# Spreading dense tiles and the samples' attention over the eight pairs of heads, with seven instead of four merge-gate blocks kept in DRAM

## The chip, the core and the metric

The kernel runs on one core of one Trainium2 chip. The metric is the device time of one execution in microseconds (us). The core has a matrix engine (TensorE, PE in the profile), a vector engine (DVE), a scalar engine (ACT), a general engine (POOL) and a queue engine (SP) that issues most of the transfers; each runs its own instructions strictly in the order in which they were written, and waits where an operand or a buffer isn't ready.

## What is computed

One layer of a decoder for a prompt of 512 tokens and for 8 samples with one new token and 1024 cached positions each. Two attentions run on the same input; the core of the reference is:

```python
h = x * (1.0 + scale[:, None, :]) + shift[:, None, :]
parts = jnp.split(h @ w_in, np.cumsum(IN_WIDTHS)[:-1], axis=-1)
(a_q, a_kc, a_vc, a_ks, a_vs, a_kw, a_vw, a_g, a_z, b_q, b_k, b_v, b_z, m_a, m_b) = parts
...
o_a = nsa_attention(...)    # compressed, selected and window branch, gated per head
o_b = moba_attention(...)   # blocks chosen by q . mean(k), plus the own block
y_a = (o_a.reshape(bsz, t, NSA_WIDTH) * jax.nn.silu(a_z)) @ w_up_a
y_b = (o_b.reshape(bsz, t, MOBA_WIDTH) * jax.nn.silu(b_z)) @ w_up_b
mixed = (jax.nn.sigmoid(m_a) * y_a + jax.nn.sigmoid(m_b) * y_b) @ w_out
x_new = layer_norm(DEEPNORM_ALPHA * x + gate[:, None, :] * mixed, ln_g, ln_b)
```

All numbers are f32; for the samples the keys and values come from paged caches through a page table.

## The kernel before

**Dense tiles.** The product with `w_in` is cut into tiles of 128 output columns. `dense` (L550) does one: 48 matmuls on two PSUM banks, `d<-hTh,hl` twice and `d<-hTl,hl` once for each of 16 pieces, because f32 is split into a high and a low part. The weights of a tile are one load of 512 KB (`raw<-w_cols`, L342, on SP, ring of 4 buffers), and each half is split by an ACT cast (L310) and a subtraction on DVE or POOL (L231) into `hl` (ring of 3). `SEQ` fixes the order of all tiles. Tile names: bq, bk, bv, bz are query, key, value and gate path of the second attention (0 to 3), q, z those of the first, ma and mb the two merge gates (0 to 7; "m3" means ma3 and mb3), g the output gate's four parts (each two loads `raw<-ada_g` of the same ring).

**Prompt attention.** `attend(pi)` (L1112) does the pair of heads pi of 0 to 7: `prepare` (L957) loads the bias band from `band_d`, a table in DRAM; then `score` (L1001, PE writes bank s, DVE adds the band, L1012, ACT takes the exponential, L1016), `turn` (L1021, transposes), `value` (L1035). Pairs 0 to 3 also have the compressed branch (`cmp_score`, matmuls `s<-ck,q`). `band_d` itself is written once, by one transfer of 3 MB on POOL's queue (L940), while the compression is worked out.

**The samples' attention.** `dec_a` (L1177) and `dec_b` (L1252) run through a list of loads, with two buffers: 4 items of 16 selected-key pages (`raw<-slck`, 64 KB each, L721 on SP, one transfer for each page), 2 window-key items (`wink`), 16 items of 4 pages `mobk` (256 KB each), twice two gathers of values by POOL (`slcv`) and one window-value load (`winv`), and 16 items of 4 pages `mobv` (256 KB each). An item can be loaded when the item two before it has been used.

**What sets the order.** `merge` (L177) takes generators of work and always steps the one with the smallest share done. For each pair of heads three are merged: `attend(pi)`, whose total is `ATT[pi]`, the samples' attention up to the share `DEC_SHARE[pi]`, and the dense tiles `FILLS[pi + 1]`. What is left of the samples' attention runs with `FILLS[9]` after the last pair. `FILLS[0]` goes with the compression before. The tables thus set the order of every engine's instructions, SP's loads too.

**Merge gates.** `gen_m` (L648) puts ma and mb of a block through a tanh. A block computed while the pairs of heads still run has no place in SBUF: its halves go through `mg` (two buffers) to `m_d` in DRAM (L658, 260 KB a half), and are loaded again (L1332, 520 KB a block) when the pool `fm` has been opened after pair 7. Blocks of `FILLS[9]` stay in SBUF.

Of the kernel before, what the change touches and what calls it, by code (L numbers as in the profile page):

```python
# [33 lines left out]
        + [f"{n}{t}" for t in range(4) for n in ("bq", "bz", "bv", "bk")]  # L34
        + [f"{n}{c}" for c in range(8) for n in ("ma", "mb")])
FILLS = [["ks", "vs", "ag", "vw", "q0", "bq2", "kw", "q1", "q2", "q3"],
         ["bq0", "bq1"],
         ["bq3", "bv0"],
         ["z0", "bk0", "m0"],
         ["bv1", "z1", "m1", "bv2"],  # L40
         ["bk1", "m2"],
         ["z2", "bk2", "m3"],
         ["bv3", "z3", "bk3"],
         ["bz0"],
         ["bz1", "bz3", "bz2", "g0", "m4", "g1", "g2", "m5", "m6", "g3", "m7"]]
DEC_SHARE = [0.09, 0.15, 0.28, 0.31, 0.37, 0.45, 0.52, 0.66]
DEC, DEC_PACE = 50000.0, 0.875
PHIS = 49353.58399999998
ATT = [20400, 20000, 17000, 47040, 10800, 5250, 7500, 9000]
SECOND = [3, 4, 6, 7]  # L50
LIM = 0, 384, 384, 768
NORM_N = 512
# [124 lines left out]
def merge(*flows):  # L177

    while True:
        live = [f for f in flows if f.live]  # L180
        if not live:
            return
        min(live, key=Flow.share).step()
# [7 lines left out]
def build(tc, A):  # L191
# [44 lines left out]
    with ExitStack() as es:  # L236
# [441 lines left out]
        def fill_cost(names):  # L678
            return max(1.0, sum(2 * DENSE if n[0] == "m" else 1000 if n[0] == "g" else 1700 if n == "ag" else 1 if n == "ks" else DENSE for n in names))
# [432 lines left out]
        def attend(pi):  # L1112
            js = jobs_of(pi)
            if pi < 7:
                prepare(pi + 1)
            for k, j in enumerate(js):
                ex = []
                if pi < 4 and k == 0:
                    ex = [(cmp_score, pi)]
                if pi < 4 and k == 1:  # L1120
                    ex = [(cmp_turn, pi)]
                yield from step(j, ex)
            if pi == 7:
                for _ in range(2):
                    yield from step(None)
# [187 lines left out]
        def part(until):  # L1313
            while fa.live and fa.share() < until:
                d = fa.done
                fa.step()
                yield fa.done - d

        done = 0.0
        for pi in range(8):  # L1320
            merge(Flow(attend(pi), ATT[pi]), Flow(part(DEC_SHARE[pi]), max(1.0, (DEC_SHARE[pi] - done) * DEC)),
                  Flow(fills(FILLS[pi + 1]), fill_cost(FILLS[pi + 1])))
            done = DEC_SHARE[pi]
        at_es.close()
# [370 lines left out]
```

## Time and profile before

| | |
|---|---|
| median of three runs | 663.61 us (657.27 to 663.81) |
| profiled execution | 660.91 us |
| its span | 659.1 us |
| PE busy | 619.0 us, 94% |
| DVE, ACT, POOL busy | 310.5, 295.2, 287.3 us |
| mean granted clock of TensorE | 0.974 |
| moved by DMA | 124.77 MB |

The span runs from the first to the last instruction of the profiled execution. A window gives the busy time of each engine in a stretch of it, the granted clock of TensorE there (1.00 is 2.4 GHz, 0.50 is 1.2 GHz) and the share of time in which the 16 DMA engines were at work. In a chain of waits each piece is what the next one waited for.

### The profile page before, as it was taken

The page shows a single profiled execution, that of the slowest core. Times are in us where ns is not written, and L with a number is a line of the kernel's source. Part 1 is how long each engine was busy: PE and PEld are TensorE (multiplying, and loading weights), DVE is VectorE, ACT ScalarE, POOL GpSimd, SP SyncE. Part 2 cuts the span into 40 slices and gives each one's busy share as a digit, 9 for nine tenths or more (in the row PEclk, how much of TensorE's full clock was granted, in tenths as well). Part 3 has the DMA queues.
Part 4 walks back from the last instruction along what each step waited for, and adds up shares of the span by engine and source line. Part 5 has one row for each costly group of instructions (what it writes and reads, how often), then busy time and mean ns, then how long its engine had stood idle before and what let it go on. Part 6 is the DMA issues. An engine that isn't in the chain of part 4 may idle for free.

```text
span 659.1 us, 13320 instructions
## 1 busy us (share of the span) xinstructions
PE 619.0 (94%) x4747; PEld 518.1 (79%) x4747; DVE 310.5 (47%) x800; ACT 295.2 (45%) x679; POOL 287.3 (44%) x328
## 2 busy tenths in 40 slices
PE   6999999999979799999999899998988999999993
PEld 4778999999959578776879679865635998999672
DVE  1465543532572664335355446744431145545177
ACT  2248455544443545444445446645433353433521
POOL 1105466542352433442364544445432264655746
PEclk9998999999998969999999989999998999999998
DMA  8895554539953594699775563168977344345102
GB/s 309 337 293 188 167 179 144 171 98 97 165 186 104 155 360 141 216 310 311 245 229 196 196 237 97 49 220 312 304 264 288 100 153 137 96 129 188 68 24 106
DMA packets 64132, 124.77 MB, mean 189 GB/s; under 512 B 8142, under 2 KB 28368, under 8 KB 63521
## 3 DMA queue, kind: packets, MB, share of 16 engines
q1 hardware_dynamic: 61954, 116.58, 52.9%
q0 software_dynamic: 2112, 7.34, 6.3%
q8 instruction: 37, 0.61, 0.4%
q14 instruction: 29, 0.24, 0.1%
HBM read 112.76 MB, written 11.13 MB: 188 GB/s over the span
## 4 chain that ended last, share of the span: by engine, by line
PE 66%; DMA 6%; SPq 3%; DVE 3%; issue 2%; ACT 1%; POOL 1%; POOLq 0%; ACTq 0%; DVEq 0%
PE d L199 40%; PE s L199 9%; PE e L199 7%; DMA raw<-mobv 3%; PE pt L1025 3%; SPq L721 2%; PE o L202 2%; PE o L199 2%; PE pt L199 1%; PE e L202 1%; DMA raw<-slcv,vidx 1%; DMA raw<-winv 1%; DVE xt L1488 1%; DMA craw<-cmp 1%; SPq L717 0%
## 5 line engine op out<-in xcount | busy, mean ns | idle before, releaser
L199 PE MATMUL d<-hTh,hl 128*128 128x260 f32 (+1 forms) x1408 | 273.1, 290 | 1.4 <-DVE hl L231 1.1
L199 PEld LDWEIGHTS d<-hTh,hl 128*128 128x128 f32 (+1 forms) x1408 | 221.4, 189 | 16.8 <-issue 9.4
L199 PE MATMUL d<-hTl,hl 128*128 128x260 f32 (+1 forms) x704 | 201.4, 287 | 0.0
L199 PEld LDWEIGHTS d<-hTl,hl 128*128 128x128 f32 (+1 forms) x704 | 133.2, 189 | 3.2 <-issue 2.5
L231 POOL TENSOR_TENSOR hl<-raw,hl 128x512 fp32r<-128x512 f32 x56 | 73.5, 1314 | 104.2 <-ACT hl L310 99.6
L310 ACT CAST hl<-raw 128x512 fp32r<-128x512 f32 (+1 forms) x111 | 67.8, 615 | 76.1 <-PE d L199 62.6
L1018 POOL TENSOR_SCALAR p<-p,sm,gp 128x512 f32<-128x512 f32 (+1 forms) x64 | 40.0, 626 | 95.8 <-DVE sm L1017 91.2
L1016 ACT ACTIVATE p<-s,sm 128x512 f32<-128x512 f32 (+1 forms) x96 | 50.8, 530 | 65.9 <-PE pt L1025 54.0
L231 DVE TENSOR_TENSOR hl<-raw,hl 128x512 fp32r<-128x512 f32 (+1 forms) x55 | 53.5, 974 | 49.4 <-ACT hl L310 47.6
L199 PE MATMUL d<-yh,hl 128*128 128x260 f32 x256 | 46.3, 282 | 0.0
L1025 PE MATMUL pt<-cst,p 128*128 128x128 f32 x240 | 40.3, 282 | 1.5 <-DVE pp L1030 0.8
L199 PEld LDWEIGHTS d<-yh,hl 128*128 128x128 f32 x256 | 39.7, 188 | 1.0 <-issue 0.4
L199 PE MATMUL s<-kd,q 128*128 128x512 f32 (+1 forms) x96 | 35.1, 366 | 4.6 <-ACT p L1016 4.6
L1010 DVE TENSOR_REDUCE sm<-s 128x1 f32<-128x256 f32 (+1 forms) x48 | 16.9, 354 | 44.9 <-PE s L199 43.9
L1025 PEld LDWEIGHTS pt<-cst,p 128*128 128x128 f32 x240 | 27.8, 142 | 11.5 <-issue 5.8
L1018 POOL TENSOR_SCALAR p<-p,sm,cst 128x512 f32<-128x512 f32 (+3 forms) x32 | 19.5, 611 | 38.1 <-DVE sm L1017 37.9
L199 PE MATMUL d<-yl,hl 128*128 128x260 f32 x128 | 36.0, 282 | 0.0
L199 PE MATMUL s<-u,w1h 128*128 128x256 f32 (+1 forms) x160 | 33.5, 301 | 1.2 <-ACT u L793 0.7
L1012 DVE CUSTOM_DVE_ANT_0 s<-s,band 128x256 f32<-128x256 f32 (+1 forms) x48 | 17.3, 362 | 35.2 <-PE s L199 24.8
L199 PEld LDWEIGHTS s<-kd,q 128*128 128x128 f32 x96 | 18.6, 194 | 17.8 <-ACT p L1016 8.6
L231 POOL TENSOR_TENSOR u<-craw,u 128x512 fp32r<-128x512 f32 x16 | 21.3, 1331 | 24.8 <-ACT u L828 24.8
L199 PE MATMUL s<-kd,qx 128*128 128x512 f32 (+1 forms) x96 | 31.5, 330 | 0.0
(425 smaller groups left out, 1167.3 us busy)
## 6 DMA issues: line engine op xcount, KB each, us to landing
raw<-w_cols SPq DMA_DIRECT2D x46, 512.0 KB
raw<-mobk SPq DMA_DIRECT2D x64, 256.0 KB
raw<-mobv SPq DMA_DIRECT2D x64, 256.0 KB
u<-ada_ss SPq DMA_DIRECT2D x16, 512.0 KB
craw<-cmp SPq DMA_DIRECT2D x64, 128.0 KB
raw<-slck SPq DMA_DIRECT2D x64, 64.0 KB
raw<-ada_g SPq DMA_DIRECT2D x8, 512.0 KB
raw<-w_up SPq DMA_DIRECT2D x8, 512.0 KB
```

Of the source, the lines that this page charges most:

```text
L199: i = mmraw(out, lhsT, rhs, start=start, stop=stop, skip_group_check=True)
L202: i = mmraw(out, lhsT, rhs, start=start, stop=stop, skip_group_check=True)
L231: (nc.gpsimd if eng == "p" else nc.vector).tensor_sub(out, x, f32(hi))
L310: nc.scalar.copy(h, src)
L721: dyn.append(nc.sync.dma_start(out, A[name][bass.ds(page, 1)].rearrange("a p c -> p (a c)")))
L1010: nc.vector.tensor_reduce(sm[:, 0:1], s[:, :b], axis=AX, op=OP.min)
L1012: nc.vector.tensor_tensor_reduce(out=s[:, b:n], in0=s[:, b:n], in1=j.band[:, 256 - (n - b):], scale=1.0, scalar=top, op0=OP.add, op1=OP.mi ...
L1016: nc.scalar.activation(pr, s[:, :n], AF.Exp, scale=-1.0, bias=sm[:, 1:2], accum_out=sm[:, 2:3])
L1018: nc.gpsimd.tensor_scalar(pr, pr, sm[:, 3:4], j.gate(i), op0=OP.mult, op1=OP.mult)
L1025: nc.tensor.transpose(p[:, k * 128:k * 128 + 128], j.p[i][:, kb * 128:kb * 128 + 128], ident)
L1488: add(xt[tt][:, c], xt[tt][:, c], u)
```

## The change

Three tables, and nothing else:

```diff
--- before.py
+++ after.py
@@ -34,19 +34,19 @@
         + [f"{n}{t}" for t in range(4) for n in ("bq", "bz", "bv", "bk")]
         + [f"{n}{c}" for c in range(8) for n in ("ma", "mb")])
 FILLS = [["ks", "vs", "ag", "vw", "q0", "bq2", "kw", "q1", "q2", "q3"],
-         ["bq0", "bq1"],
-         ["bq3", "bv0"],
-         ["z0", "bk0", "m0"],
-         ["bv1", "z1", "m1", "bv2"],
-         ["bk1", "m2"],
-         ["z2", "bk2", "m3"],
-         ["bv3", "z3", "bk3"],
-         ["bz0"],
-         ["bz1", "bz3", "bz2", "g0", "m4", "g1", "g2", "m5", "m6", "g3", "m7"]]
-DEC_SHARE = [0.09, 0.15, 0.28, 0.31, 0.37, 0.45, 0.52, 0.66]
+         ["bq0", "m0", "bq3", "bq1"],
+         ["bv0", "m1", "bk0", "bv1"],
+         ["z0", "m2", "m3"],
+         ["m4", "z1", "m5"],
+         ["bk1", "bv2", "z2"],
+         ["bk2", "bv3", "bk3"],
+         ["z3", "bz0"],
+         ["bz1", "m6"],
+         ["bz3", "bz2", "g0", "g1", "g2", "g3", "m7"]]
+DEC_SHARE = [0.15, 0.3, 0.44, 0.56, 0.6, 0.64, 0.74, 0.845]
 DEC, DEC_PACE = 50000.0, 0.875
 PHIS = 49353.58399999998
-ATT = [20400, 20000, 17000, 47040, 10800, 5250, 7500, 9000]
+ATT = [17100] * 4 + [7100] * 3 + [11000]
 SECOND = [3, 4, 6, 7]
 LIM = 0, 384, 384, 768
 NORM_N = 512
```

Before, blocks m0 to m3 are computed among the pairs of heads and wait in DRAM; now m0 to m6, which is six more stores `m_d<-mg` of 260 KB and three more loads of 520 KB. Of the samples' attention, 66% of the steps were done with the pairs of heads; now 84.5%. After the last pair, ten entries with bz1, bz3, bz2, four blocks of m and the gates were left; now bz3, bz2, the four gates and m7.

The order moves on all engines from the first tile after the compression on. Three places, word for word.

PE, where the first score of pair 0 stands. Names: `s<-kd,q` is a score, `s<-ck_88` the compressed branch's scores, `d<-hTh,hl` and `d<-hTl,hl` a dense tile, `e<-xc`, `e<-cvd,u` and `e<-cst_72,pr` steps of the samples' compressed branch (`dec_cmp`, L887, and `new_scores`, L872). Before:

```order
L199 MATMUL d<-hTl,hl 128x260
L199 MATMUL d<-hTh,hl 128x260 x2
L199 MATMUL d<-hTl,hl 128x260
L199 MATMUL s<-kd,q_1970 128x512
L199 MATMUL s<-ck_88,q_1970 128x64
L199 MATMUL d<-hTh,hl 128x260 x2
L199 MATMUL d<-hTl,hl 128x260
```

and in the changed program:

```order
L199 MATMUL e<-xc,cstd 128x64
L912 MATMUL e<-cst_72,xc 64x128
L199 MATMUL e<-cvd,u 128x128 x4
L199 MATMUL e<-cst_72,pr 128x1 x2
L199 MATMUL s<-kd,q_1970 128x512
L199 MATMUL s<-ck_88,q_1970 128x64
```

Before, this score stood behind five whole dense tiles and part of the sixth (bk0), counted from the compression's end, and the steps of `dec_cmp` lay apart among them; now it stands right behind these steps, with bq0, ma0 and half of mb0 ahead.

SP, at the loads of the band (L961) and of the first selected-key pages (slck). Before:

```order
L721 DMA craw<-cmp 128x256
L342 DMA raw<-w_cols 128x1024 x6
L572 DMA ok<-ev 128x520
L961 DMA band<-band_d 128x2x256 x2
L717 TENSOR_LOAD ptt
L721 ISA
L721 DMA raw<-slck 128x128
```

and in the changed program:

```order
L721 DMA craw<-cmp 128x256
L342 DMA raw<-w_cols 128x1024 x4
L961 DMA band<-band_d 128x2x256 x2
L717 TENSOR_LOAD ptt
L721 ISA
L721 DMA raw<-slck 128x128
```

Two weight loads fewer stand ahead of the band; the 64 page loads follow it directly in both, with no weight load among them.

PE, at the last value item (`e<-raw,tp`, 4 pages mobv) and the gates' matmuls (`s<-raw,cs`). Before:

```order
L199 MATMUL s<-raw,cs 32x512
L202 MATMUL s<-raw,cs 32x512 x3
L199 MATMUL e<-raw,tp 32x512
L202 MATMUL e<-raw,tp 32x512 x3
L199 MATMUL d<-hTh,hl 128x260 x2
L199 MATMUL d<-hTl,hl 128x260
```

and in the changed program, from the third gate on:

```order
L199 MATMUL s<-raw,cs 32x512
L202 MATMUL s<-raw,cs 32x512 x3
L199 MATMUL o<-pp,v_5298 64x512
L202 MATMUL o<-pp,v_5298 64x512
L202 MATMUL o<-pp,v_5298 64x384 x2
L202 MATMUL o<-pp,v_5298 64x256 x2
L202 MATMUL o<-pp,v_5298 64x128 x2
L199 MATMUL s<-raw,cs 32x512
L202 MATMUL s<-raw,cs 32x512 x3
L199 MATMUL d<-hTh,hl 128x260 x3
L199 MATMUL d<-hTl,hl 128x260
```

Before, half of mb4 and the six tiles ma5, mb5, ma6, mb6, ma7 and mb7 stood behind the last value item, with the fourth gate between mb6 and ma7; now only ma7 and mb7 do, behind pair 7's last values and the fourth gate.

## Rows read from the trace of the kernel before

**Rows 1.** Page, parts 1 and 2: TensorE's sum and its granted clock in 40 slices.

```profile
PE 619.0 (94%) x4747; PEld 518.1 (79%) x4747; DVE 310.5 (47%) x800; ACT 295.2 (45%) x679; POOL 287.3 (44%) x328
...
PEclk9998999999998969999999989999998999999998
```

**Rows 2.** Windows: length, busy us of each engine, granted clock, DMA share, GB/s.

```profile
195.80:206.00 10.20, 10.19 (x57) 8.30 (x58) 2.87 (x10) 3.08 (x8) 1.23 (x2) 0.70 0.38 107
206.00:244.00 38.00, 33.72 (x218) 25.54 (x217) 20.93 (x63) 17.11 (x46) 13.18 (x16) 0.87 0.69 235
...
360.00:400.00 40.00, 36.36 (x405) 29.50 (x405) 19.47 (x64) 19.19 (x51) 19.48 (x23) 0.96 0.61 211
...
440.00:505.00 65.00, 57.14 (x404) 31.93 (x402) 23.52 (x86) 27.42 (x76) 25.32 (x33) 0.97 0.86 299
505.00:545.80 40.80, 40.80 (x344) 39.82 (x341) 12.84 (x13) 16.73 (x34) 15.47 (x14) 1.00 0.46 152
sum 350.00, PE 334.05 PEld 261.52 DVE 158.00 ACT 165.49 POOL 141.65; mean PE 47.72 PEld 37.36 DVE 22.57 ACT 23.64 POOL 20.24
```

**Rows 3.** Groups of instructions on PE from 145.7 to 195.8: count, busy us, mean ns.

```profile
L199 PE MATMUL d<-hTh,hl 128*128 128x260 f32 x218 | 41.7, 287 | 1.1 <-DVE hl L231 1.1
L199 PE MATMUL d<-hTl,hl 128*128 128x260 f32 x109 | 30.8, 282 | 0.0
```

**Rows 4.** Tile band_d: its one issue (start us) and its time to landing.

```profile
L940 POOL DMA_DIRECT2D band_d<-bs x1: 1104/1104/1104, 146.9 to 146.9; - x1
...
DMA to landing us min/median/max: 36.5/36.5/36.5
```

**Rows 5.** Timeline of SP's queue, 140 to 232: start, us from first to last, issue.

```profile
183.49 0.90 SPq L961 DMA_DIRECT2D band<-band_d  x2
184.93 39.75 SPq L721 DMA_DIRECT2D raw<-slck  x64
...
227.03 0.43 SPq L342 DMA_DIRECT2D raw<-w_cols  x1
```

**Rows 6.** Timeline of PE, start and us: around the first page item and before z1.

```profile
195.81 1.03 PE L199 MATMUL e<-raw,zn 128*32 128x512 f32 x1 [3.50 <-DMA raw<-slck]
...
197.93 0.80 PE L199 MATMUL d<-hTh,hl 128*128 128x260 f32 x2
```

**Rows 7.** The same view, 228 to 241.

```profile
231.14 1.09 PE L199 MATMUL e<-ew 33*128 33x512 f32 x2 [2.17 <-ACT pp L1028]
...
237.25 0.78 PE L199 MATMUL d<-hTh,hl 128*128 128x260 f32 x2
```

**Rows 8.** Chain of waits, in order of time: start, us, what.

```profile
376.36 5.43 DMA raw<-slcv,vidx
...
446.31 5.88 DMA raw<-mobv
...
485.00 3.80 DMA raw<-mobv
...
495.80 8.16 DMA raw<-mobv
...
534.19 35.62 PE d L199 x288
...
577.73 10.06 PE d L199 x84
```

**Rows 9.** Windows, same columns as Rows 2: the value loads, and the band table's write.

```profile
432.50:503.60 71.10, 63.64 (x455) 37.45 (x454) 27.20 (x97) 30.40 (x82) 27.09 (x35) 0.98 0.85 293
150.00:165.00 15.00, 15.00 (x129) 14.77 (x127) 3.59 (x10) 6.52 (x17) 4.11 (x4) 1.00 0.98 97
```

**Rows 10.** Timeline of ACT, start and us: a weight split that waits for its load.

```profile
173.16 0.62 ACT L310 CAST hl<-raw 128x512 fp32r<-128x512 f32 x1 [2.06 <-DMA raw<-w_cols]
```

**Rows 11.** Page, part 5: the two halves of a weight split.

```profile
L231 POOL TENSOR_TENSOR hl<-raw,hl 128x512 fp32r<-128x512 f32 x56 | 73.5, 1314 | 104.2 <-ACT hl L310 99.6
L310 ACT CAST hl<-raw 128x512 fp32r<-128x512 f32 (+1 forms) x111 | 67.8, 615 | 76.1 <-PE d L199 62.6
```


## The prediction

> **What bounds the kernel now.** I read the page first. TensorE is busy 619.0 us of 659.1 [rows 1], so whatever this change does must be read from PE's idle stretches and from the slices in which its granted clock falls from 2.4 to 1.2 GHz. The windows come next [rows 2]: from 195.8 to 545.8 (ma7 and mb7 start at 534.19 in the chain [rows 8], and 96 of that piece's 288 matmuls later the up projections begin, which the change doesn't touch) PE is busy 334.05 of 350.0 us. So 15.95 us are idle, and nearly all of that lies in three windows: 206 to 244, 360 to 400 and 440 to 505. What the clock costs in a window is its length times what lacks of 1.00: 3.06 us in 195.8 to 206, 4.94, 1.60 and 1.95 in the three named, 11.55 in sum. That makes 27.5 us that a better order after 195.8 could win. Then the timelines and the chain say what each loss is. First, SP's queue [rows 5]: the table band_d, issued at 146.9, lands 36.5 us later [rows 4], the band loads go at 183.49, behind them 64 page loads hold SP for 39.75 us, and the next weights are issued at 227.03; z1 starts at 237.25 [rows 7]. PE runs out of dense tiles in between: it idles before 231.14 for 2.17 us, and is then at half clock (the first pieces of z1 show twice the time of two matmuls). Second, PE waits for the gathered values (376.36, 5.43 us) [rows 8]. Third, the 14 last value items come in a stretch that the DMA engines fill to 85%, at 293 GB/s [rows 9], and the chain passes from item to item: 5.88, 3.80, 8.16 us [rows 8].
>
> **What the change costs: the start.** Up to 145.7 us the programs are alike. In both, PE's first item of selected-key pages starts when its 16 page loads are there, at 195.81 [rows 6], because SP issues them only behind the band, and the band only behind band_d. Before, PE has by then done 218 + 109 = 327 dense matmuls since 145.7 [rows 3]. Counted in the changed order, 168 stand ahead of the same item: the first scores stand so early that the second one waits for a bank that comes free only when the band is there, some 10 us later. The attention done by then is the same. A dense matmul takes 10.06 / 84 = 0.120 us [rows 8], so 159 matmuls, 19.0 us, are left over. This is the one term that I read as nearly certain; PE is idle here for about that long, and all else on this engine queues behind.
>
> Two weight loads fewer stand ahead of the band. While band_d is written the engines are at work 98% of the time and move 97 GB/s [rows 9]: alone, 3 MB would take 3.146 / 0.097 = 32.4 us instead of 36.5, so the two loads can bring the band and all page loads forward by 0 to 4.1 us. I take 1.0, since some weight loads remain.
>
> Here a rule speaks on how much. ACT waits until 173.16 for a weight load [rows 10] of the time in which band_d is written, and 150 to 165 shows no more than band_d's rate [rows 9]. The Trainium skill (DMA: Bandwidth & Descriptors, Queues, rings and completion order) says that each DMA engine takes turns between the queues it has work for, packet by packet. By that rule SP's loads would get through at once and delay band_d all along, and fewer of them would give the whole 4.1 us: the sum below would end 3.1 us lower. The row, with no more than 97 GB/s moved, doesn't show the weights coming through early.
>
> **What it gives: 195.8 to 250.** The 159 matmuls now lie in the stretch where PE ran dry. Weights of seven tiles are loaded ahead of the band (two loads fewer than before, where nine were), which leaves 336 - 168 = 168 matmuls, 20.1 us, against 106 that ran in before's 195.8 to 237.25. They reach about as far as mb1's weights, the first behind the page loads, which can be ready at the 237.25 at which z1 could start. So the 4.28 us idle and 4.94 us of clock go; I leave 0 to 3 us for mb1's weights, taken with the next window. The half clock right behind the first item (3.06) stays, since PE idles longer ahead of it now.
>
> **250 to 400.** By the order, 909 dense matmuls lay between the first page item and the first of the 14 value items; now 1218. That covers more waits, among them the gathers': of 3.64 idle and 1.60 of clock I keep 1.5 (0 to 5.2). Six stores to m_d and three more loads add 3.1 MB; at 232 to 300 GB/s that is 10 to 13 us of the engines, in stretches that leave 30% and more of them free; 1.0 us for all that and mb1's weights (0 to 4).
>
> **The value items.** From the first to the last of 14 they took 71.1 us, with 132 dense matmuls among them. Now 198 lie there: 66 more, 7.9 us; some scores, values and transposes (about 5.2 us by count) moved out, so PE's work in the stretch grows by 2.7. Its work before was 63.64 busy less 1.4 of clock, 62.2, so 64.9 now. The same 14 items and about as many weight, gate and gate-block loads pass. At before's rate the stretch stays 71.1 (6.2 us lost); at a full share it needs 71.1 x 0.85 = 60.4 and PE sets it (0 lost). Items stand more evenly now, one for each 4.6 us of PE's work, near the 3.80 to 5.88 us of an item with two buffers; I take the middle, 3.0, in place of 7.86 + 1.95.
>
> **Behind the last value item.** Before, 312 dense matmuls ran here without a wait, and loads had all their time. Now the gates' loads fill the ring of four, and ma7's weights are issued only when the third gate's matmuls are done. Estimated from rows: a transfer of 3.80 to 5.88 us (chain, a value item; a weight load is half as large), ACT 0.62 and POOL 1.31 for the split [rows 11], less about 3.3 us that pair 7's values and the fourth gate take: 2.4 to 4.5. I take 3.0 (1 to 4.5).
>
> **The sum.** 350.0 + 19.0 left over - 27.5 + 3.1 (clock kept) + 1.5 + 1.0 + 3.0 + 3.0 - 1.0 = 352.1 us from 195.8 on, 2.1 us more than before. Against its own execution, 660.91, this gives 663.0. The median of the runs shown is 663.61, so it stands between; their spread of 6.5 us is about 1%, which is what a measurement of this kernel can tell from no change. All losses at their low end, with the band 4.1 early, give 350.0 + 19.0 - 27.5 + 3.1 + 1.0 - 4.1 = 341.5, so 652.4; a wait inside a started matmul counts as busy in the windows, and may hide 2 us more of gain. All at their high end: 344.6 + 5.2 + 4.0 + 6.2 + 4.5 = 364.5, so 675.4.
>
> **The rivals.** *Everything after the start is hidden.* The even order keeps PE fed to the end, band and page loads come up to 4 us earlier. For it: 309 more dense matmuls to hide waits with, and a full share of DMA that would allow 60.4 us for the value items. Against it: two buffers, and a fixed order with no slack. It gives 651 to 655. *The value items stay bound by DMA, and the start is not repaid.* One mechanism: 14 MB of values with two buffers run at no more than 293 GB/s however they are placed, so the stretch takes 71.1 us again, and its PE work, larger than before, doesn't shorten it; behind it only two tiles are left where before 312 matmuls ran, with ma7's weights late. With the gathers' wait also partly there (3), this gives 344.6 + 3 + 1 + 6.2 + 4.5 - 1 = 358.3, so 669. It decides against the change from 67 us in that stretch on. For it: 5.88, 3.80 and 8.16 us pieces of the chain. Against it: the 85% contain waits of SP for PE. *PE is late at the first page item.* ACT and DVE are held by the band too, and the splits of bq1 and bv0 stand behind their waiting instructions; if weights come 6 us late after the band, the clock stays low with them: 663 + 6 + 1.5 = 670. *The change shifts losses only* is my forecast.
>
> **How the numbers follow.** The forecast, losses moved from the end to the start and the sum within 1%, 0.44. All hidden, 0.24. DMA-bound values or a late restart, 0.32. The range leaves out 1 in 10 on each side: 651 at the low end, where the first rival reaches, and 674 near the sum of all high ends. The forecast's own range is 657 to 668. Faster by over 1%: 0.24; within 1%: 0.44; slower: 0.32.
>
> **What would show it.** PE idle for 10 us or more between 170 and 188, and a second wait before 195.8; the band's load issued at 180 to 184; no idle at 228 to 237. The first page item at 191 to 196 with 168 dense matmuls behind it; the value stretch at 65 to 71 us; a wait of ma7 for its weights; the up projections at 543 to 553. It is wrong if PE isn't stopped by the band (then the kernel is faster by up to 19 us), or if a new wait shows between 250 and 400.

## The result

The changed kernel takes 665.05 us in the median (20 runs, 662.34 to 670.07), the kernel before 661.38 us (20 runs, 654.36 to 665.69, on the same chip): a ratio of 1.0083, with 95% from 1.0059 to 1.0106. By this ratio it is 0.8% slower, some 5.5 us; the two medians lie 3.7 us apart. The forecast was 663.0 us and no difference that can be told: the time lies in the range, but the difference is there, and it is a loss. The profiled execution of the changed kernel is 663.52 us with a span of 661.8, against 660.91 and 659.1 of before.

The page of the profile after, TensorE's sum and its granted clock, as [rows 1]:

```profile
PE 617.3 (93%) x4747; PEld 517.7 (78%) x4747; DVE 311.0 (47%) x800; ACT 294.1 (44%) x679; POOL 290.7 (44%) x328
...
PEclk9999999998669999999999999999999989999997
```

The clock now falls to 0.6 in two slices of 16.5 us, from 165 to 198 us, where it was 0.9 before; the 0.6 that before had from 231 to 247 is gone. The timeline of SP's queue from 140 to 250 us of the changed kernel, as [rows 5] (start, length, and how many issues):

```profile
180.59 0.90 SPq L961 DMA_DIRECT2D band<-band_d  x2
182.05 41.33 SPq L721 DMA_DIRECT2D raw<-slck  x64
...
226.22 0.38 SPq L342 DMA_DIRECT2D raw<-w_cols  x1
```

The tile band_d of the changed kernel: its one issue, who waited for it, and its landing, as [rows 4]:

```profile
L940 POOL DMA_DIRECT2D band_d<-bs x1: 1104/1104/1104, 145.2 to 145.2; - x1
...
  ACT mg L656: 12.8, 1
  DVE s L1012: 10.0, 1
...
DMA to landing us min/median/max: 3.0/19.1/35.3
```

The write starts 1.7 us earlier than before, by a stretch in which both programs are alike, and takes 1.2 us less. The first page item of the samples' attention starts 2.5 us earlier. PE's timeline of the changed kernel from 164 to 200 us, as [rows 6] (brackets: idle time ahead, and what ended it):

```profile
168.56 0.80 PE L199 MATMUL s<-kd,q 128*128 128x512 f32 x1 [1.03 <-DVE q L970]
...
185.03 0.58 PE L199 MATMUL s<-kd,q 128*128 128x256 f32 x1 [7.33 <-ACT p L1016]
...
193.28 1.06 PE L199 MATMUL e<-raw,zn 128*32 128x512 f32 x1 [3.25 <-DMA raw<-slck]
```

The first scores (over 512 and over 384 columns) are done from 168.56 on; the third, over 256 columns at 185.03, waits until the first has got its band and gone through ACT. That is decided by the band: its loads go at 180.59, DVE's addition waits 9.97 us for them and starts at 183.55, ACT's exponential follows at 184.19. Then the page loads are waited for. Windows of the changed kernel from the first page item to the up projections, the columns of [rows 2]:

```profile
193.30:206.00 12.70, 12.70 (x81) 10.70 (x85) 4.48 (x17) 3.77 (x10) 2.22 (x4) 0.76 0.38 108
206.00:244.00 38.00, 37.74 (x288) 30.13 (x283) 19.34 (x62) 21.02 (x54) 14.87 (x17) 1.00 0.69 242
244.00:360.00 116.00, 115.94 (x949) 91.99 (x948) 52.53 (x161) 54.44 (x138) 48.30 (x55) 1.00 0.75 251
360.00:400.00 40.00, 40.00 (x416) 36.46 (x415) 17.90 (x60) 19.23 (x51) 14.91 (x20) 1.00 0.56 185
400.00:456.00 56.00, 54.18 (x429) 48.57 (x428) 33.28 (x98) 33.74 (x85) 30.31 (x35) 1.00 0.26 81
456.00:525.30 69.30, 63.98 (x483) 42.30 (x481) 25.41 (x91) 28.46 (x79) 24.61 (x33) 1.00 0.88 292
525.30:548.70 23.40, 22.15 (x161) 16.29 (x161) 11.41 (x10) 10.98 (x22) 13.27 (x11) 0.93 0.73 264
sum 355.40, PE 346.69 PEld 276.44 DVE 164.36 ACT 171.63 POOL 148.49; mean PE 49.53 PEld 39.49 DVE 23.48 ACT 24.52 POOL 21.21
```

Here 8.71 us are idle, and the clock costs 3.05 us in the first window and 1.64 in the last: 13.4 us lost, where before 27.5 were. Without the losses the stretch holds 342.0 us of work, before 322.5: 19.5 us were left over by the start. So 355.4 us replace 350.0. The middle won what it was to win (37.74 of 38 busy, was 33.72; 40.00 of 40, was 36.36); what remains lost lies at the start's clock, between 400 and 456 (1.82 idle), in the value items (5.32 idle) and behind them. The chain of waits of the changed kernel there, as [rows 8]:

```profile
477.91 7.18 DMA raw<-mobv
...
502.94 5.08 DMA raw<-mobv
...
514.29 4.22 DMA raw<-mobv
...
520.59 4.70 DMA raw<-mobv
...
530.97 3.74 DMA raw<-w_cols
534.73 0.63 ACT hl L310
535.43 1.28 POOL hl L231
536.76 8.77 PE d L199 x71
```

Value pages are waited for four times; then ma7's weights, issued at 530.97 when the third gate is done, are on the path until ma7 starts at 536.76. From the up projections (548.7; before 545.6) to the end the two take 113.1 and 113.5 us.

### The profile page after: what moved, and what is told of

Same layout as the page of the kernel before. It is cut to its first block, busy times and chain, and to the rows that moved or that the text cites. A ratio compares the mean times of both kernels' runs of the same rounds, so it can differ in the third digit from the quotient of the medians.

```text
span 661.8 us, 13320 instructions
## 1 busy us (share of the span) xinstructions
PE 617.3 (93%) x4747; PEld 517.7 (78%) x4747; DVE 311.0 (47%) x800; ACT 294.1 (44%) x679; POOL 290.7 (44%) x328
## 4 chain that ended last, share of the span: by engine, by line
PE 60%; DMA 11%; SPq 3%; DVE 3%; issue 2%; ACT 1%; POOL 1%; POOLq 0%; ACTq 0%
PE d L199 36%; PE s L199 8%; PE e L199 6%; DMA band_d<-bs 5%; PE pt L1025 3%; DMA raw<-mobv 3%; SPq L721 2%; PE o L202 2%; PE o L199 2%; DMA raw<-w_cols 1%; PE pt L199 1%; PE e L202 1%; SPq L717 1%; DVE xt L1488 1%; DMA craw<-cmp 1%
## 5 line engine op out<-in xcount | busy, mean ns | idle before, releaser
L199 PE MATMUL d<-hTh,hl 128*128 128x260 f32 (+1 forms) x1408 | 276.2, 290 | 0.9 <-POOL hl L231 0.6
L231 DVE TENSOR_TENSOR hl<-raw,hl 128x512 fp32r<-128x512 f32 (+1 forms) x55 | 50.8, 925 | 44.0 <-ACT hl L310 39.8
L199 PEld LDWEIGHTS s<-kd,q 128*128 128x128 f32 x96 | 18.5, 193 | 16.5 <-ACT p L1016 10.9
```

Of the source, the lines that this page charges most:

```text
L199: i = mmraw(out, lhsT, rhs, start=start, stop=stop, skip_group_check=True)
L231: (nc.gpsimd if eng == "p" else nc.vector).tensor_sub(out, x, f32(hi))
```

## The experiments

One table for all. "Page item" is the start of the first item of selected-key pages in PE's timeline of the profiled execution, "to the end" the time from there to the span's end. The ratio is to the kernel before, run beside it on the same chip (659.30 to 663.03 us there). The stretch up to 145 us is not the same in every execution (last section), so stages are compared by their lengths.

| kernel | what | median us (runs) | ratio, 95% | page item | to the end |
|---|---|---|---|---|---|
| before | | 661.38 (20) | 1 | 195.8 | 463.3 |
| after | the change | 665.05 (20) | 1.0059 to 1.0106 | 193.3 | 468.5 |
| e16 | the change again | 666.02 (10) | 1.0027 to 1.0106 | 194.8 | 469.6 |
| e15 | before, m0 second in the list | 669.43 (4) | 1.0052 to 1.0173 | 195.0 | 472.9 |
| e1 | after, m0 fifth | 661.88 (10) | 0.9987 to 1.0066 | 194.2 | 466.3 |
| e10 | after's start, rest of before | 673.43 (4) | 1.0161 to 1.0261 | 193.4 | 475.2 |
| e14 | after, half the rows in the band | 650.22 (4) | 0.9778 to 0.9904 | 177.8 | 467.9 |
| e14b | before, the same | 656.52 (10) | 0.9909 to 0.9987 | 190.6 | 463.9 |
| e2 | after, band written one pair earlier | 671.03 (4) | 1.0082 to 1.0227 | 202.1 | 466.1 |
| e17 | after, band written from SP | 662.53 (10) | 0.9994 to 1.0082 | 187.2 | 472.9 |
| e18 | e1 with it | 664.29 (12) | 1.0037 to 1.0095 | 193.7 | 468.8 |
| e7 | after, band in two transfers | 672.70 (4) | 1.0109 to 1.0321 | 194.6 | 475.0 |
| e8 | before, the same | 666.05 (10) | 1.0027 to 1.0120 | 198.1 | 467.1 |
| e9 | e1 with the same | 660.16 (10) | 0.9958 to 1.0043 | 198.5 | 457.0 |
| e12 | after, half the heads in the band | 672.10 (4) | 1.0140 to 1.0306 | 193.1 | 473.1 |
| e5 | after, band's source elsewhere | 676.06 (4) | 1.0131 to 1.0277 | 203.2 | 472.5 |
| e4 | after, m6 computed last | 668.50 (5) | 1.0029 to 1.0212 | 199.3 | 475.4 |
| e3 | after, gates earlier | 670.75 (4) | 1.0058 to 1.0197 | 199.4 | 475.2 |
| e11 | after, gates last | 672.25 (4) | 1.0091 to 1.0252 | 193.8 | 476.3 |
| e13 | e1 with gates last | 660.75 (10) | 0.9986 to 1.0058 | 194.2 | 464.3 |

**What sets the start: the place of m0 (e1, e15).** The first takes the change's start away and keeps the rest, the second puts only m0's place into the kernel before.

```diff
--- after.py
+++ e1_m0_later
-         ["bq0", "m0", "bq3", "bq1"],
-         ["bv0", "m1", "bk0", "bv1"],
+         ["bq0", "bq3", "bq1", "bv0"],
+         ["m0", "m1", "bk0", "bv1"],
--- before.py
+++ e15_m0_first
-         ["bq0", "bq1"],
-         ["bq3", "bv0"],
-         ["z0", "bk0", "m0"],
+         ["bq0", "m0"],
+         ["bq1", "bq3"],
+         ["bv0", "z0", "bk0"],
```

> The changed kernel with its two first rows of dense tiles in another order: bq0, bq3, bq1, bv0 with pair 0, and m0, m1, bk0, bv1 with pair 1 (before, m0 stood in the row of pair 0 and bv0 in that of pair 1). In the order, 326 dense matmuls instead of 168 then stand between the compression and the first selected-key item, as in the kernel before (327). Theory (the loss is made at the start, where PE waits for the band with too few tiles ahead): 158 matmuls x 0.120 = 18.9 us come back, less what the 206 to 244 stretch loses again (up to 9.2), so 5 to 10 us faster than the changed kernel, a ratio of 0.992 to 1.000 to the kernel before. Rival (the loss lies behind 440 us, in the value loads and the tail): this edit leaves that part as it is, so within 2 us of the changed kernel, ratio 1.005 to 1.011.

> The kernel before with one part of the change alone: m0 second among the tiles (rows bq0 m0, bq1 bq3, bv0 z0 bk0), all shares and totals as before. In the order, 168 dense matmuls stand ahead of the first page item, as in the changed kernel. Theory (that place of m0 makes the start's loss by itself): 19.0 us left over, of which the dry stretch at 206 to 244 gives back up to 9.2, so 8 to 14 us slower than the kernel before, first page item at 193 to 196, PE idle 7 us ahead of the third score. Rival (the start's loss is made up behind it in any case, and the late part is what decides): within 3 us of the kernel before.

PE's timeline of e15 around the same places:

```profile
186.62 0.58 PE L199 MATMUL s<-kd,q 128*128 128x256 f32 x1 [7.11 <-ACT p L1016]
...
194.95 1.06 PE L199 MATMUL e<-raw,zn 128*32 128x512 f32 x1 [3.00 <-DMA raw<-slck]
```

These are the waits of the changed kernel (7.33 and 3.25), in the tables of before but for m0: 168 dense matmuls stand ahead of the page item, and it costs 1.1%. So m0's place, with the regrouping of three rows that it needs, makes the loss of the start, without any other part of the change. In e1, the other way round, 326 stand ahead and PE has one wait there, 4.99 us for the pages. But e1 is no faster than before, and by the medians 3.2 us faster than the change, where 5 to 10 were expected. Windows of e1 behind the page item and behind the value items:

```profile
206.00:244.00 38.00, 33.46 (x183) 19.01 (x184) 22.45 (x76) 20.90 (x55) 13.26 (x18) 0.82 0.68 224
505.00:547.40 42.40, 34.15 (x203) 22.86 (x196) 10.29 (x11) 12.13 (x25) 13.79 (x13) 0.76 0.80 289
```

The 158 matmuls it did earlier (19.0 us) are missing later: 4.5 us idle and 6.8 of clock from 206 to 244, 8.3 and 10.2 at the end, 29.8 us (the clock counted over the whole window, its idle part included) against 0.3 and 7.3 in the same places of the changed kernel. From the page item to the end it saves only 2.2 us. The dense tiles are one stock; a stretch that gets more leaves another dry.

**What the later part is worth (e10).** The first two rows of `FILLS` and shares of the change, the rest from before, the tiles left out of the rows put behind.

```diff
--- after.py
+++ e10_late_of_before
-         ["z0", "m2", "m3"],
-         ["m4", "z1", "m5"],
...
+         ["z0"],
+         ["z1", "bv2"],
...
+         ["bz1", "bz3", "bz2", "g0", "m4", "g1", "g2", "m5", "m6", "g3", "m7"]]
-DEC_SHARE = [0.15, 0.3, 0.44, 0.56, 0.6, 0.64, 0.74, 0.845]
+DEC_SHARE = [0.15, 0.3, 0.305, 0.31, 0.37, 0.45, 0.52, 0.66]
-ATT = [17100] * 4 + [7100] * 3 + [11000]
+ATT = [17100, 17100, 17000, 47040, 10800, 5250, 7500, 9000]
```

> The changed kernel's rows for pairs 0 and 1, and from pair 2 on the rows, the shares of the samples' attention and the attention's totals of the kernel before, as far as the tiles already done allow (m0 to m3 in DRAM, 66% of the samples' attention with the pairs, 132 dense matmuls among the value items and 312 behind them, as before). Theory (the start loses 19 us, the later part wins some 14 of them back): the start's loss stays, the waits of before at 360 to 400 and 440 to 505 (5.2 and 9.8 us) come back and the changed kernel's 10 us there go: 3 to 7 us slower than the changed kernel, 668 to 672. Rival (the new later part, with more blocks in DRAM and a tail without cover, is what costs): faster than the changed kernel by 2 us and more.

The page item starts at 193.4 as in the changed kernel, the up projections at 555.1 instead of 548.7: the later part of the change wins 6.4 us in the profiled executions, within the 3 to 7 expected, and 8.4 by the medians, a little more. The window of e10's value items, from the first to the last, 70.2 us long:

```profile
443.20:513.40 70.20, 63.43 (x455) 37.23 (x454) 27.21 (x97) 30.93 (x84) 27.45 (x35) 0.98 0.88 297
```

So the change is a start that costs and a later part that wins, and the start is the larger.

**Is it the band? (e14, e14b).** The write of the table is made half as long: 64 of its 128 rows are written, and each band is loaded as these rows twice. The work of all compute engines stays.

```diff
-                        nc.gpsimd.dma_start(band_d[:, :, 0:384], D["band"].unsqueeze(1).to_broadcast([16, 128, 384]))
+                        nc.gpsimd.dma_start(band_d[:, 0:64, 0:384], D["band"].unsqueeze(1).to_broadcast([16, 64, 384]))
-            nc.sync.dma_start(bt, bass.AP(tensor=band_d.tensor, offset=band_d.offset + h0 * 128 * 385 + 127,
-                                          ap=[[384, 128], [hs * 128 * 385, 2], [1, 256]]))
+            for r in range(2):
+                nc.sync.dma_start(bt[64 * r:64 * r + 64], bass.AP(tensor=band_d.tensor, offset=band_d.offset + h0 * 128 * 385 + 127,
+                                          ap=[[384, 64], [hs * 128 * 385, 2], [1, 256]]))
```

> The changed kernel with half of the bias table: band_d is written for the first 64 of 128 rows of every head (1.5 MB, all 16 heads), and each band is loaded as these rows twice (one load becomes two), so the bias of half the queries is wrong. In e12_half_band, where half of the heads were left out, the write took 35.3 us as before, so its time goes by the rows of one head and not by the bytes; here it should fall to half. Theory (PE's third score, SP's page loads and the weights behind them wait for the band): it lands 17 to 20 us after its issue, the band goes at 163 to 166, the third score waits under 2 us, the first page item starts at 175 to 182 instead of 193.3, and up0 13 to 18 us earlier less what the later stretches can't follow: 8 to 14 us faster than the changed kernel. Rival (PE or SP is held by something else there): first page item at 188 or later, under 5 us faster.

> The same half table in the kernel before, so the bias of half the queries is wrong here too. If the changed kernel loses because the band finds it with fewer tiles to do, the early band is worth less here, 3 to 8 us, and the changed kernel comes within 3 us of this one. If the start has nothing to do with the loss, both gain alike and stay 4 to 5 us apart.

Tile band_d of e14, and windows of e14 around its first page item, which starts at 177.78 without a wait:

```profile
L940 POOL DMA_DIRECT2D band_d<-bs x1: 857/857/857, 144.5 to 144.5; - x1
...
DMA to landing us min/median/max: 18.1/18.1/18.1
```

```profile
162.00:177.80 15.80, 12.70 (x81) 11.79 (x79) 12.03 (x33) 7.44 (x18) 9.59 (x11) 0.78 0.54 166
177.80:206.00 28.20, 26.50 (x203) 22.59 (x203) 13.05 (x44) 13.50 (x38) 10.87 (x14) 1.00 0.36 102
206.00:244.00 38.00, 37.14 (x284) 29.77 (x283) 20.83 (x63) 20.60 (x51) 10.68 (x14) 1.00 0.75 267
```

With the write 17.2 us shorter the page item comes 15.5 us earlier, and the kernel ends 16.1 us earlier; what follows takes 467.9 us, as in the changed kernel (468.5). So most of the start's loss, 15.5 of some 19 us, was the wait for the band; the idle time in the steps of the compressed branch stays (4.6 us from 145.7 to 170, in the changed kernel 5.1). The shorter write also frees the DMA engines for weights and pages that much earlier, and e14 doesn't tell this from the earlier landing. In the tables of before the page item comes 5.2 us earlier by the same shortening, since there PE has its own work up to 190.6, and the kernel is 0.5% faster (3.4 us). So with the band early the change is 6.3 us faster than before (650.22 against 656.52), more than the 3 us expected of e14b, and with the band where it is 3.7 to 5.5 us slower. The sign hangs on that one transfer.

**Can the band come earlier? (e2, e17, e18).** e2 issues the write one pair of the compression earlier; e17 issues it from SP right behind the last load of the compression, e18 does so with e1's rows.

```diff
--- after.py
+++ e2_band_early
-BAND_AT = 3
+BAND_AT = 2
--- after.py
+++ e17_band_on_sp
-                    with tc.issue_after(D["last"].ins):
-                        nc.gpsimd.dma_start(band_d[:, :, 0:384], D["band"].unsqueeze(1).to_broadcast([16, 128, 384]))
+                    with tc.issue_after(dyn[-1].ins):
+                        nc.sync.dma_start(band_d[:, :, 0:384], D["band"].unsqueeze(1).to_broadcast([16, 128, 384]))
```

> The changed kernel with band_d written after the third pair of the compression instead of the fourth, some 17 us earlier. Theory (PE stops because the band is late): band_d lands near 165 instead of 180.5, the wait of 7.3 us at the third score goes, and the first page item starts 8 to 15 us earlier: 5 to 10 us faster than the changed kernel. Rival (the write takes the DMA engines from the compression's loads and the weights at that time, so the wait only moves ahead): the compression ends 5 to 15 us later, and the time is the same or up to 8 us longer.

> The changed kernel with band_d's write issued by SP instead of POOL, right behind the last load of the compression's rows; the table is whole. e14_half_rows showed that an early band makes the changed kernel 14 to 16 us faster than it is and 6 us faster than the kernel before with the same early band. On POOL's queue the write moves 97 GB/s in packets of 4608 B that take 743 ns each; the loads of SP's queue take 159 ns for 4096 B. If the slowness belongs to POOL's queue, the band lands in under 20 us: 650 to 654, faster than both kernels. If it belongs to the table (each engine reads one head's row again and again and writes DRAM), it lands at 180 as before and the weights behind it on the same queue come later: 666 to 674.

> e17_band_on_sp with m0 one row later, as in e1_m0_later. In e17_band_on_sp the write took its 33 to 36 us on SP's queue too, 96 GB/s, but was issued 14 us earlier, so the band went at 167.0 and the first page item at 187.2; ACT then waited 11.8 us for a weight load behind it on the same queue, and PE with it. Theory (tiles ahead of the band and the band's time cover each other): 284 dense matmuls instead of 168 ahead of the first page item, which starts at 186 to 190: 653 to 658, faster than the kernel before by 0.3 to 1.2%. Rival (the weights behind the write are what PE waits for, so more tiles ahead of the band don't help): 660 to 664, no faster than e17_band_on_sp.

In e2 the write is issued at 128.2 instead of 145.2, and the compression pays, whose loads it slows down: ACT waits 18.15 us for one of them, until 147.98. A window of e2 ahead of the dense stretch:

```profile
62.00:145.70 83.70, 74.21 (x587) 72.01 (x586) 35.65 (x55) 34.71 (x76) 42.08 (x48) 0.95 0.64 155
```

Before, PE is busy 83.17 of these 83.70 us, so the 17 us of lead cost 9 us of idle here (the wait goes on to 149.96, 13.36 us in all), and the page item comes 8.8 us later than in the changed kernel. In e17 the table is there at 167.03 and the page item comes at 187.2, yet no more is won. ACT's timeline of e17 at a weight split, and PE's at a step of the samples' compressed branch:

```profile
168.42 0.62 ACT L310 CAST hl<-raw 128x512 fp32r<-128x512 f32 x1 [11.84 <-DMA raw<-w_cols]
```

```profile
170.20 0.39 PE L912 MATMUL e<-cst,xc 128*64 128x128 f32 x1 [9.93 <-DVE im L905]
```

The weights now wait for the write, ACT for the weights, and PE for what stands behind on ACT and DVE. 6 us earlier at the page item, 4.4 later from there to the end: 662.53 us, 0.4% over before with an interval that reaches it. With m0 moved too (e18) the order costs again what e1's did (32.52 of 38 us busy from 206 to 244), and the early write is of no use: on SP six weight loads, where e17 has four, now stand ahead of the band's loads, which go at 180.40, and the page item comes at 193.7 instead of the 186 to 190 expected.

**Can it be made shorter? (e7, e8, e9, e12).** The write in two halves of eight heads (on the changed kernel, on before, on e1), and half the heads alone, where pairs 4 to 7 read the heads of 0 to 3.

```diff
-                        nc.gpsimd.dma_start(band_d[:, :, 0:384], D["band"].unsqueeze(1).to_broadcast([16, 128, 384]))
+                        for hb in (slice(0, 8), slice(8, 16)):
+                            nc.gpsimd.dma_start(band_d[hb, :, 0:384], D["band"][hb].unsqueeze(1).to_broadcast([8, 128, 384]))
--- after.py
+++ e12_half_band
+                        nc.gpsimd.dma_start(band_d[0:8, :, 0:384], D["band"][0:8].unsqueeze(1).to_broadcast([8, 128, 384]))
-            h0, hs = (pi, 4) if pi < 4 else (2 * pi, 1)
+            h0, hs = (pi, 4) if pi < 4 else (2 * pi - 8, 1)
```

> The changed kernel with band_d written by two transfers one behind the other, heads 0 to 7 first (1.5 MB, all that pairs 0 to 3 read), heads 8 to 15 second. The bytes and the place are the same. Theory (PE, SP's page loads and the weights behind them all wait for the band): the first half lands about 18 us after its issue, so band and page loads go at 163 to 168 instead of 180.6, the wait of 7.3 us at the third score goes, the first page item starts at 175 to 185 instead of 193.3: 8 to 14 us faster than the changed kernel, 650 to 657. Rival (the second half holds the DMA engines until 182 all the same, and the page loads land no earlier): within 3 us of the changed kernel.

> The kernel before with the same two transfers for band_d. It has 327 dense matmuls to do meanwhile, so PE doesn't wait for the band's landing but for the pages (3.5 us) and, at 228 to 237, for weights behind the page loads. Theory: page loads and weights go 10 to 17 us earlier, so both waits shrink, 4 to 9 us faster than the kernel before. Rival (the first wait only moves ahead of the scores, and the weights' place isn't decided by the band): within 2 us of the kernel before.

> m0 one row later (as in e1_m0_later) and band_d in two halves together. If the band's time and the tiles ahead of it are one and the same loss, the two gains don't add: 326 dense matmuls cover the band in any case, so only the page loads and the weights behind them come earlier, and the dry stretch at 206 to 244 (idle 4.5, clock 6.8 us in e1_m0_later) shrinks: 4 to 9 us faster than e1_m0_later, 653 to 658. If they are two losses, it is faster than e7_band_halves by 3 us and more.

> The changed kernel with band_d written for heads 0 to 7 alone (1.5 MB); pairs 4 to 7 then read the bands of heads 0 to 7, so their logits have the wrong bias. All else is as in the changed kernel. This is what e7_band_halves was to do: there both halves landed together, 36 us after their issue. Theory (PE, SP's page loads and the weights behind them wait for the band): it lands 17 to 19 us after its issue, band and page loads go at 163 to 168 instead of 180.6, the wait at the third score is under 1 us, the first page item starts at 174 to 185: 8 to 14 us faster than the changed kernel. Rival (something else releases the page loads or PE, the chain of the compressed branch or the weights): the first page item at 188 or later, less than 5 us faster.

Tile band_d of e7 (two issues; the largest landing is that of the write):

```profile
L941 POOL DMA_DIRECT2D band_d<-bs x2: 1100/1130/1160, 144.5 to 145.6; - x2
...
DMA to landing us min/median/max: 3.2/5.5/36.6
```

The first half was to land in half the time. In e8 the two land after 36.0 and 38.2 us, in e7 the later one after 36.6, and the half in e12 alone after 35.3. So these four runs didn't shorten the wait they were made to shorten, and say nothing for or against it; e9 is level with before, as e1 is, and why e8 is 0.7% slower than before stays open. e7 and e12 are slower than the changed kernel, probably for another reason: their page items come within 1.3 us of its own, and the altered program also got another order among the value items, with the gates' loads issued at 527.46 and 526.38 instead of 521.92; the chains wait 4.49 and 4.47 us for them there. That a late gate costs the end is also the reading of e11 below.

**Is it ACT's wait? (e5).** In the changed kernel ACT too waits 12.8 us, at a gate block's tanh, for the band's source to be free. The source goes into another ring:

```diff
-            bs = st.tile([16, 384], F32, name="bs")
+            bs = pair("kd", F32)[:16, 0, :384]
```

> The changed kernel with the source of band_d in a buffer of its own (of the ring kd), so that ACT's second write to mg no longer waits for band_d to be read out; orders as in the changed kernel but for a few rows. Theory (the band itself holds PE's third score, and ACT's wait of 12.8 us lies beside that): within 1 us of the changed kernel. Rival (ACT, held by the memory that mg shares with band_d's source, is what stops PE): the wait at the third score shrinks, 3 to 7 us faster.

ACT's wait is gone; DVE's for the band is 12.1 us and the score waits still. So ACT's wait isn't what stops PE. The time itself says nothing: that ring is in use at the start, where PE is busy 50.45 of the first 62 us instead of 54.3, and the write starts 9 us later.

**The value items and what is behind them (e4, e3, e11, e13).** m6 behind the last pair; the gates ahead of bz2; the gates behind m7, with the changed start and with e1's.

```diff
--- after.py
+++ e4_m6_sbuf
-         ["bz1", "m6"],
-         ["bz3", "bz2", "g0", "g1", "g2", "g3", "m7"]]
+         ["bz1"],
+         ["bz3", "bz2", "g0", "g1", "g2", "g3", "m6", "m7"]]
+++ e3_gates
+         ["bz3", "g0", "g1", "g2", "g3", "bz2", "m7"]]
+++ e11_gates_last
+         ["bz3", "bz2", "m7", "g0", "g1", "g2", "g3"]]
```

> The changed kernel with m6 taken out of the row of pair 7 into the last row, ahead of m7: it stays in SBUF, two stores and one load of m_d fewer (1.04 MB), 102 instead of 198 dense matmuls among the value items and 192 instead of 96 behind them. Theory (cover is what counts): the value items wait longer, by up to 96 x 0.120 = 11.5 us of missing cover that comes back behind them, where nothing waits but ma6's weights; 0 to 5 us slower than the changed kernel. Rival (the three more blocks' way through DRAM is what costs): 1 to 3 us faster.

> The changed kernel with the four gates one tile earlier in the last row: bz3, g0 to g3, bz2, m7. Theory (ma7 waits for its weights because their load stands behind the gates in the ring of four): the wait of 3.7 us for the load and 1.9 us for the split goes, and bz2 covers the last pair's values: 2 to 4 us faster than the changed kernel. Rival (the gates' 2 MB then meet the value loads while the DMA engines are full, and the last value items get later by as much): 0 to 1 us.

> The changed kernel with the gates behind m7 in the last row. Then 270 instead of 198 dense matmuls stand among the value items and 24 instead of 96 behind them. Since the value items took 58 us with 102 as with 198 matmuls among them, the transfers set that stretch, and tiles put into it are free up to what PE waits there. Theory: 72 x 0.120 = 8.6 us move into it, of which the 5.3 us that PE waited are free, and ma7's wait goes: 4 to 7 us faster than the changed kernel, 658 to 661. Rival (the gates' four last loads then stand ahead of the up projections' weights in the ring of four, and PE waits there instead): within 2 us of the changed kernel.

> m0 one row later (e1_m0_later) and the gates behind m7 (e11_gates_last). Theory (two separate losses, one at the start, one at the end): e1_m0_later's tail, 8.3 us idle and 10.2 us of clock from 505 to 547, shrinks by 8 us and more: 651 to 655, faster than the kernel before by 0.8% or more. Rival (the tail's wait moves to the up projections' weights): 658 to 662.

Windows of e4, from the first to the last value item and on to the up projections:

```profile
462.50:530.30 67.80, 57.70 (x424) 32.25 (x423) 22.93 (x88) 26.54 (x74) 24.16 (x33) 1.00 0.89 310
530.30:561.70 31.40, 30.60 (x218) 29.69 (x219) 11.54 (x11) 12.79 (x25) 14.90 (x13) 0.84 0.49 177
```

96 matmuls fewer lie among the items (102 for 198), 11.5 us of work, and the stretch takes 67.8 us for the changed kernel's 68.8 (456.5 to 525.3): the transfers set its length, and the dense tiles in it were covered. Taken out, they come on top: from the last item to the up projections 31.4 us for 23.4, page item to end 6.9 us longer. (The medians, 668.50 and 665.05, don't tell the two kernels apart, since e4's interval holds that of the change.) In e3 the gates' loads compete with the values, and the same stretch takes 75.3 us:

```profile
456.50:525.30 68.80, 63.48 (x479) 41.96 (x478) 25.41 (x91) 27.96 (x77) 24.11 (x33) 1.00 0.88 293
```

```profile
463.40:538.70 75.30, 67.26 (x471) 39.74 (x473) 24.15 (x88) 28.05 (x77) 21.57 (x31) 0.93 0.87 291
```

The first row is the changed kernel's, the second e3's. The rate is the same, so e3's stretch moves some 1.8 MB more (the rate times the length), and it is longer by that much; both its theory and its rival expected no loss. In e11 the gates stand last. Its stretch, with 270 dense matmuls, takes 69.3 us, 68.42 of them with PE busy, so the tiles fill what was idle; the loss comes behind it. (The 58 us in the expectation of e11 count from the third item on.) The chain of waits of e11 there:

```profile
532.09 5.90 DMA raw<-ada_g
...
544.32 3.43 DMA raw<-w_up
...
548.84 3.67 ACT yh L1346 x7
```

The weights of the up projections queue behind the gates' loads in the ring of four, and the up projections start at 557.1 instead of 548.7: a loss, where the theory expected a gain and the rival no change. With e1's start (e13) the same order is no worse than e1's own (660.75 and 661.88), as its rival expected, and both are level with before. No kernel that computes all of the reference came out faster than before.

## Why the prediction was right and wrong

The forecast was losses that only move, and a sum of +2.1 us called no change; the kernel is 0.8% slower. The mechanism was right, and the step that failed is one term of the sum: the value items, put at 3.0 us and measured at 5.32, because their transfers and not PE set the stretch. The terms in order:

*The start, 19.0 us left over.* Right: 19.5. The mechanism, the band that stops a score, is shown by e14 (shorter write: most of the loss gone) and its cause by e15 (m0's place); it is the third score that waits, not the second. The idle time came a little otherwise than told: 7.33 us in one wait where 10 were expected, and 5.1 of idle ahead of it, from 145.7 to 170, in the steps of the samples' compressed branch that now stand without dense tiles between them.

*The band 1.0 us earlier.* Right: the page item came 0.8 us earlier beyond the 1.7 by which this execution was ahead already. By the rule of the Trainium skill that was weighed there (DMA: Bandwidth & Descriptors, Queues, rings and completion order) two loads fewer would have taken up to 4.1 us off the write; it became 1.2 shorter. In other runs too the write lands after 36.3 to 36.7 us with four weight loads issued during it (before, e1, e13) and after 35.3 to 35.4 with two (the change, e15, e16), so the measurement stands against the whole 4.1.

*Clock kept, 3.1.* Right, 3.05. *206 to 400.* 1.5 us were left for the gathers, 0.3 lost; 1.0 for mb1's weights and the traffic to DRAM, and 1.8 lost, but from 400 to 456, where the DMA engines are at work 26% of the time and PE waits for ACT (0.88, 0.39, 0.33 and 0.15 us).

*The value items: this term was mis-sized.* 3.0 us was the middle between nothing lost and the 6.2 of before's length; measured 5.32. The stretch took 68.8 us, near the 71.1 of "at before's rate" and far from the 60.4 of a full share. e4 and e10 show why: with 102, 132 or 198 dense matmuls among the items it takes 67.8, 70.2 and 68.8 us, so its length goes with the transfers and not with PE's spacing. The rival of value items bound by DMA (6.2 lost) had this step right, though its 293 GB/s is no ceiling: e4's stretch moves 310. (The stretch of 71.1 us holds all 16 value items, not 14; for the first two the loads land before it.)

*Behind the last value item, 3.0.* Right: 1.25 idle and 1.64 of clock, with ma7's weights late as told.

*The sum.* 19.5 of work, less 27.5, plus 13.4 lost (11.6 foretold), less 0.8 is +4.6 us, where +2.1 was foretold. Of these 2.5 us the value items are 2.3, the work 0.5 and the band 0.2; the other losses came out 0.5 smaller than told. The profiled times differ by 2.6 only because this execution was 1.7 us ahead at the band's issue; e16's, where the write starts at 146.9 as in before, is 5.3 us over before's, and the ratio's 5.5 us, with an interval of 3.9 to 7.0, agree with both. That two misses of 0.5, the work's and the other losses', cancel is luck. The sum had the right sign, and a loss of 2 us was called no change, by a spread of 6.5 us that was read as the limit of what can be told; 20 runs of each tell half a per cent. With the value items at the bound that the row showed the sum would have been 5.3 us, 0.8% slower.

What stays open: why the merge, given m0 second in the list, puts pair 0's scores so far ahead was not tried apart; nor whether the DMA engines' rate or the two buffers set the stretch of the value items (e3, longer at the same rate, speaks for the rate).

## What to carry to other kernels

Filling work is one stock: before moving it, list the stretches that can't do without it, and count what is left there; here the later stretches gave back 14 us, and the start, stripped of 19, could not. An order that puts a consumer ahead of work that needs nothing turns a hidden transfer into a wait for everything behind it, so ask of each first score, first page or first gate what its slowest operand is and when that lands. A stretch whose length stays the same with half the matmuls in it is set by its transfers: work put there is covered as long as it adds little to the transfers (e3's gates did add), and its losses count at the measured rate, not at a full one.

## What was not expected of the hardware

The write of the band table takes 36.5 and 35.3 us for 3 MB, 36.6 in two transfers of eight heads issued 1.1 us apart, and 35.3 for eight heads alone; with half the rows of every head it takes 18.1. From 145.7 to 170 the DMA engines are at work 94% of the time in the changed kernel and 54% with eight heads alone (e12). On SP's queue it runs at the same rate, 98 GB/s from 145 to 160 us. So in these runs its time goes by the rows of one head and not by its bytes, as if each head had its own engine, and a split along the heads didn't shorten it.

The stretch before the change is not the same in each execution: the granted clock from 60 to 80 us was 1.00 in one profile of the changed kernel and 0.91 in the other (e16), 0.91 in that of before and 0.66 in e3's and e4's, and the write of the band table was issued at 145.2, 146.9, 146.9, 150.6 and 150.4 us. Such a difference is as large as the whole effect here, which is why stages were compared by their own lengths.
